# A float32 encoder trunk on one core: the first pair of feed-forward output tiles by eight plain block products instead of seven Winograd ones, with the input loaded in another order

## The chip, the cores and the metric

The kernel runs on 1 core of one Trainium2 chip, as one launch. The metric is device microseconds of that launch, the median of several runs. Engine names: PE is TensorE (its weight loads are PEld), DVE is VectorE, ACT is ScalarE, POOL is GpSimd, SP is SyncE, which here only issues transfers.

## What is computed

A two-layer encoder over 512 tokens of 1024 channels, all in float32. Only the first feed-forward block and the norm ahead of it are touched by the change:

```
for l in range(2):
    h = rmsnorm(x, ffn1_norm[l])
    x = x + 0.5 * (silu(h @ w_gate) * (h @ w_up)) @ w_down      # 1024 -> 2816 -> 1024
    ... mixer: windowed pooling, a 2-D Fourier transform, differential attention; x = x + concat @ w_out
    ... a second SwiGLU block of the same shape
out = rmsnorm(x, final_norm)
```

## The kernel before

The input lies transposed: eight tiles `X[k]` of 128 channels by 512 tokens. Every product is float32 made of three passes: an operand is split into a rounded part `hi` (ACT, line 103) and the remainder `lo` (DVE, line 104), and hi·hi, hi·lo and lo·hi are accumulated in PSUM. The norm's factor per token is not applied to the input of a product. Only the gain per channel is (`scaled`); the sums of squares run beside it (`squared`), and `end` makes the factor `r` by a reciprocal square root written out in DVE operations.

**Units.** A feed-forward block has 2816 / 128 = 22 hidden tiles, taken in pairs: a `Unit` computes the gate and up columns of one pair. It is a 2x2 block product. The blocks of the weights are a11, a12, a21, a22 (rows: the two tiles of the pair; columns: even and odd `X[k]`), each 128x1024 values or 512 KB, and those of the input are the halves `c0` (tokens 0 to 255) and `c1` (256 to 511) of even and odd `X[k]`. Seven Winograd products replace the eight plain ones. Each product is 24 matmuls of 128x256 (line 386 to 388: four pairs `p`, gate and up, three passes), so a unit is 168 matmuls. Its operands are sums of blocks. On the input's side `PairNorm.scaled` makes them on ACT and DVE once for all 11 units. On the weights' side transfers make them: a block is loaded by SP, and GpSimd issues a transfer that adds a second block onto it in SBUF (line 160 for a sum from the start, line 175 for the next sum once the tile has been split). So one tile `t` of a unit holds a21+a22, then that plus a11, then that plus a12.

**Order.** A list of raw tiles and a list of recipes are made ahead (which raw tile is split when, and what is added onto it then). `load` issues transfers up to five raw tiles ahead into 7 stage buffers; `produce` splits; `operand` keeps the splits three ahead of PE in 4 buffers. A unit is `head` (products 5 and 1), then the unit before it ends (`tail`), then `middle`; PSUM's 8 banks are given out in turn. Four units (chunk one of 4, 4 and 3) are followed by the down products `dn`. In the code all this stands in program order; a planner inside the framework then writes each engine's queue from that order and from its own estimate of when operands are ready, and each queue runs strictly in order.

**Start.** SP loads the small constants, then `X[0]`, `X[1]`, a11 of unit 0, `X[2]`, `X[3]`, the first tile `t`, and the rest. For the first unit products 1 and 5 are swapped, since product 1 needs the plain block a11 alone. After its `head` eight squares go to ACT and six of their seven additions to POOL.

Of the kernel before, what the change touches and what calls it, by code (L numbers as in the profile page):

```python
# [33 lines left out]
P = 128  # L34
D = 1024
S = 512
# [30 lines left out]
def build(tc, xt, gu, dn, qk, wv, wfa, wo, pw, fw, small, lamv, alibi, dft_c, dft_s, out):  # L67
# [3 lines left out]
    with (  # L71
# [50 lines left out]
        for l in range(L):  # L122
            for n in range(2):
                i = 2 * l + n
                if n:
                    src = {f"P{h}": qk[l, h] for h in range(NH)}
                    src |= {"V0": wv[l, 0], "V1": wv[l, 1], "A": wfa[l, 1], "F": wfa[l, 0]}
                    src |= {"W0a": wo[l, 0], "W1a": wo[l, 1], "W2": wo[l, 2], "W3": wo[l, 3]}
                    for x in ORDER:
                        if x in src:  # L130
                            for z in range(2):
                                operand_of(raw(src[x][:, z * 1024 : (z + 1) * 1024]), eng=V if x in ON_VECTOR else G)
                for c0, c1 in CHUNKS:
                    tail = []
                    for u in range(c0, c1):
                        a11, a21, a22, a12 = [gu[i, u][:, q * 1024 : (q + 1) * 1024] for q in range(4)]
                        if raws:
                            t, t11 = raw(a21, plus=a22), raw(a11)
                        else:
                            t11, t = raw(a11), raw(a21, plus=a22)  # L140
                        t12, t22 = raw(a12), raw(a22)
                        head = [(t, a11), (t11, a21)]
                        for x, then in (head if recipes else head[::-1]) + tail + [(t, a12), (t11, None), (t12, None)]:
# [114 lines left out]
        class Norm:  # L258
# [13 lines left out]
            def squared(self, k):  # L272
# [4 lines left out]
                else:  # L277
                    (V if k == KT - 1 else G).tensor_tensor(self.acc, self.acc, sq, ADD)
# [7 lines left out]
        class PairNorm(Norm):  # L286
# [6 lines left out]
            def scaled(self, k):  # L293
# [5 lines left out]
                b1, b2 = self.b.pop(k - 1), self.b.pop(k)  # L299
                c0, c1 = slice(0, TH), slice(TH, S)  # L300
# [13 lines left out]
                self.x[k // 2] = res  # L314
# [57 lines left out]
        class Unit:  # L372
# [5 lines left out]
            def product(self, q, j, start, stop):  # L378
                wh, wl = operand()
# [10 lines left out]
            def head(self, swapped=False):  # L390
                self.qe, self.qa = bank("qe"), bank("qa")
                for q, j in ((self.qa, 1), (self.qe, 5)) if swapped else ((self.qe, 5), (self.qa, 1)):
                    self.product(q, j, True, True)
# [36 lines left out]

        def ffn(nm, nxt, first=False):
            for c0, c1 in CHUNKS:
                act, last = [], None
                for u in range(c0, c1):
                    unit = Unit(nm)
                    unit.head(first and u == 0)
                    if first and u == 0:
                        for k in range(KT):
                            nm.squared(k)
# [315 lines left out]
        pos[2] = 1  # L755
        for k in range(KT):
            nm.scaled(k)
# [104 lines left out]
```

## Time and profile before

| | |
|---|---|
| median of 3 runs | 1875.59 us (1872.73 to 1879.64) |
| the profiled execution | 1877.81 us, of which span 1876.0 us |
| mean granted TensorE clock | 0.982 of full speed |
| PE busy | 1774.7 us of the span |
| DVE, ACT, POOL busy | 1360.3, 851.9, 320.6 us |
| moved by transfers | 265.01 MB, mean 141 GB/s |

The span runs from the first to the last instruction of the profiled execution; the 1.8 us beside it lie outside. A busy PE counts matmuls that overlap, so that the number of matmuls in a stretch and the distance between their starts say more than the busy share.

### The profile page before, as it was taken

To read this page: it belongs to the slowest core of one execution; us is meant where nothing else is said; L and a number is where in the kernel's file an instruction comes from. 1 tells how busy PE (TensorE), PEld (TensorE's weight loads), DVE (VectorE), ACT (ScalarE), POOL (GpSimd) and SP (SyncE) were. 2 spreads that over 40 slices of the span, in tenths; PEclk is the share of its full clock that TensorE was granted. 3 is DMA by queue.
4 is the path that set the end of the run, shared out by engine and by line. 5 is a ranking of instruction groups with operands and counts; after the bars stand their busy time and mean duration, and the time that the engine had idled before them with its cause. 6 is when DMAs were issued, how large, how long until landed. Compare 5 with 4: busy or idle time off the path is not lost.

```text
span 1876.0 us, 27955 instructions
## 1 busy us (share of the span) xinstructions
PE 1774.7 (95%) x11225; PEld 1603.5 (85%) x11225; DVE 1360.3 (73%) x1956; ACT 851.9 (45%) x1189; POOL 320.6 (17%) x282
## 2 busy tenths in 40 slices
PE   5899999999879999999999999999996989999997
PEld 4898989987668999989989899898775889899896
DVE  6675765789779874855798567478987897567474
ACT  6342533448545442534555234243773554244243
POOL 3101101032322101101031010113232220010101
PEclk9899999999989999999999999999998999999998
DMA  8666867532213866857678577573322267586561
GB/s 231 150 169 137 204 165 156 138 120 85 65 42 78 188 161 147 211 151 155 161 154 195 142 167 189 129 180 124 93 71 56 65 140 197 128 193 177 127 166 45
DMA packets 76738, 265.01 MB, mean 141 GB/s; under 512 B 8640, under 2 KB 10688, under 8 KB 76608
## 3 DMA queue, kind: packets, MB, share of 16 engines
q0 software_dynamic: 25344, 92.29, 29.1%
q1 hardware_dynamic: 48096, 167.25, 27.7%
q10 hardware_dynamic: 3168, 3.68, 0.7%
q8 instruction: 88, 1.44, 0.3%
q14 instruction: 42, 0.34, 0.1%
HBM read 261.09 MB, written 2.10 MB: 140 GB/s over the span
## 4 chain that ended last, share of the span: by engine, by line
PE 69%; DVE 12%; issue 7%; DMA 5%; ACT 5%; POOL 2%; SPq 0%; DVEq 0%; ACTq 0%; POOLq 0%
PE dn L107 7%; PE dn L108 7%; PE dn L109 7%; DMA st<-in_gu 5%; PE qg L386 4%; PE qg L387 4%; PE qg L388 4%; PE qe L386 3%; PE qe L387 3%; PE qe L388 3%; PE qa L388 3%; PE qa L386 3%; PE qa L387 3%; DVE lo L104 2%; ACT hi L103 2%
## 5 line engine op out<-in xcount | busy, mean ns | idle before, releaser
L103 ACT ACTIVATE hi<-st 128x1024 fp32r<-128x1024 f32 (+2 forms) x455 | 469.2, 1036 | 668.0 <-PE dn L108 214.8
L104 DVE TENSOR_TENSOR lo<-st,hi 128x1024 fp32r<-128x1024 f32 (+2 forms) x423 | 511.5, 1213 | 179.4 <-ACT hi L103 178.3
L108 PE MATMUL dn<-al,hi 128*128 128x512 f32 x704 | 274.6, 390 | 0.0
L109 PE MATMUL dn<-ah,lo 128*128 128x512 f32 x704 | 274.1, 389 | 0.0
L107 PE MATMUL dn<-ah,hi 128*128 128x512 f32 x704 | 272.1, 392 | 0.8
L175 POOL DMA_DIRECT2D st<-in_gu x132 | 120.7, 914 | 680.3 <-DVE lo L104 606.2
L386 PE MATMUL qe<-xh,hi 128*128 128x256 f32 x704 | 203.3, 289 | 20.0 <-ACT hi L103 10.3
L386 PE MATMUL qg<-xh,hi 128*128 128x256 f32 x704 | 201.3, 286 | 8.1 <-DVE w L404 7.7
L387 PE MATMUL qe<-xh,lo 128*128 128x256 f32 x704 | 202.6, 288 | 2.2 <-DVE lo L104 2.2
L388 PE MATMUL qe<-xl,hi 128*128 128x256 f32 x704 | 202.1, 287 | 1.8 <-DVE xl L104 1.8
L387 PE MATMUL qg<-xh,lo 128*128 128x256 f32 x704 | 200.8, 285 | 2.8 <-DVE lo L104 2.8
L388 PE MATMUL qg<-xl,hi 128*128 128x256 f32 x704 | 200.6, 285 | 0.0
L452 DVE SCALAR_TENSOR_TENSOR x<-dn,x 128x512 f32<-128x512 f32 x96 | 66.1, 689 | 163.2 <-PE dn L109 163.2
L107 PEld LDWEIGHTS dn<-ah,hi 128*128 128x128 f32 x704 | 131.3, 188 | 33.1 <-ACT ah L103 7.1
L386 PEld LDWEIGHTS qe<-xh,hi 128*128 128x128 f32 x704 | 137.9, 196 | 23.9 <-ACT hi L103 16.0
L108 PEld LDWEIGHTS dn<-al,hi 128*128 128x128 f32 x704 | 132.2, 188 | 29.0 <-DVE al L104 2.4
L109 PEld LDWEIGHTS dn<-ah,lo 128*128 128x128 f32 x704 | 132.2, 188 | 26.8
L386 PEld LDWEIGHTS qg<-xh,hi 128*128 128x128 f32 x704 | 136.4, 194 | 9.4 <-DVE w L404 7.6
L387 PEld LDWEIGHTS qe<-xh,lo 128*128 128x128 f32 x704 | 137.9, 196 | 4.0 <-DVE lo L104 3.1
L388 PEld LDWEIGHTS qe<-xl,hi 128*128 128x128 f32 x704 | 138.0, 196 | 2.4 <-DVE xl L104 2.0
L387 PEld LDWEIGHTS qg<-xh,lo 128*128 128x128 f32 x704 | 136.5, 194 | 3.0 <-DVE lo L104 3.0
L388 PEld LDWEIGHTS qg<-xl,hi 128*128 128x128 f32 x704 | 136.6, 194 | 0.0
(252 smaller groups left out, 3979.1 us busy)
## 6 DMA issues: line engine op xcount, KB each, us to landing
st<-in_gu SPq DMA_DIRECT2D x176, 512.0 KB, 4.5
st<-in_gu POOLq DMA_DIRECT2D x176, 512.0 KB, 5.6
st<-in_dn SPq DMA_DIRECT2D x64, 512.0 KB, 4.3
st<-in_dn SPq DMA_DIRECT2D x32, 384.0 KB, 3.3
st<-in_qk SPq DMA_DIRECT2D x16, 512.0 KB, 3.6
st<-in_wo SPq DMA_DIRECT2D x16, 512.0 KB, 3.7
st<-in_wv SPq DMA_DIRECT2D x8, 512.0 KB, 3.9
st<-in_wfa SPq DMA_DIRECT2D x8, 512.0 KB, 3.7
```

The costliest lines, as they stand in the source:

```text
L103: A.activation(hi, src, AF.Copy)
L104: (lo_eng or V).tensor_tensor(lo, src, f(hi), SUB)
L107: T.matmul(o, lh, rh, start=start, stop=False)
L108: T.matmul(o, lh, rl, start=False, stop=False)
L109: T.matmul(o, ll, rh, start=False, stop=stop)
L175: G.dma_start(t[:, 0:w], then, accum_op=ADD)
L386: T.matmul(o, wh[:, s], xh, start=start and p == 0 and z == 0, stop=False, **k)
L387: T.matmul(o, wl[:, s], xh, start=False, stop=False, **k)
L388: T.matmul(o, wh[:, s], xl, start=False, stop=stop and p == NK - 1 and z == 1, **k)
L452: V.scalar_tensor_tensor(X[m], b, 0.5, X[m], MUL, ADD)
```

## The change

The first unit becomes a `FirstUnit`. It multiplies the four plain weight blocks with plain halves of the input, eight products of 24 matmuls: a11 with even `X`, a12 with odd `X`, a21 with even, a22 with odd, each with `c0` and `c1`. Its weight blocks need no added transfers, and each is split once. The plain halves of the input are scaled and split directly from `X` (`plain`, 16 of them, each an ACT and a DVE operation of 128x256); twelve of them stay and serve the later units, four are used by the first unit alone. The operands that are sums (`sums`, by `joined`) are made in program order behind the first unit's first two products. The squares stand behind its last product, with all additions on DVE instead of six on POOL; `end` and the multiplication by `r` stand in its `tail`. SP's order is: constants, a11, the `c0` halves of the four even `X` (128 KB each), their `c1` halves, a12, the four odd `X` whole, a21, a22, and then the second unit's tiles. All other units are as before.

```diff
-                        if raws:
-                            t, t11 = raw(a21, plus=a22), raw(a11)
-                        else:
-                            t11, t = raw(a11), raw(a21, plus=a22)
+                        if not raws:
+                            for x in (a11, a12, a21, a22):
+                                operand_of(raw(x))
+                            continue
+                        t, t11 = raw(a21, plus=a22), raw(a11)
...
-        for k in range(KT):
+        load(1)
+        for c in range(2):
+            for k in range(0, KT, 2):
+                nc.sync.dma_start(X[k][:, c * TH : (c + 1) * TH], xt[k][:, c * TH : (c + 1) * TH])
+        load(2)
+        for k in range(1, KT, 2):
             nc.sync.dma_start(X[k], xt[k])
-            if k % 2:
-                load(min(k // 2 + 1, 2 + (k > 6)))
+        load(RAWS)
...
-            def squared(self, k):
+            def squared(self, k, eng=G):
...
-                    (V if k == KT - 1 else G).tensor_tensor(self.acc, self.acc, sq, ADD)
+                    (V if k == KT - 1 else eng).tensor_tensor(self.acc, self.acc, sq, ADD)
...
+                self.x[k // 2] = self.joined(b1, b2)
+
+            def joined(self, b1, b2, res=None):
                 c0, c1 = slice(0, TH), slice(TH, S)
                 ta, tb = g(name="ta"), g(name="tb")
                 V.tensor_tensor(ta[:, c0], b1[:, c0], b1[:, c1], SUB)
                 V.tensor_tensor(ta[:, c1], b1[:, c1], b2[:, c1], SUB)
                 V.tensor_tensor(tb[:, c0], ta[:, c1], b1[:, c0], SUB)
                 V.tensor_tensor(tb[:, c1], b2[:, c0], tb[:, c0], ADD)
-                one = g(F32R, name="xo")
-                split(b1[:, c0], one[:, c0], one[:, c1])
-                res = {1: (one[:, c0], one[:, c1])}
-                for src, js in ((ta, (5, 7)), (tb, (6, 4)), (b2, (2, 3))):
+                src = [(ta, (5, 7)), (tb, (6, 4))]
+                if res is None:
...
+                for src, js in src:
                     hi, lo = g(F32R, name="xh"), g(F32R, name="xl")
                     split(src, hi, lo)
                     for j, c in zip(js, (c0, c1)):
                         res[j] = hi[:, c], lo[:, c]
-                self.x[k // 2] = res
+                return res
+
+            def plain(self, k, c):
+                gain = sm[:, self.c + k : self.c + k + 1]
+                s, c0, c1 = slice(c * TH, (c + 1) * TH), slice(0, TH), slice(TH, S)
+                o = g(F32R, name="xo")
+                A.activation(o[:, c0], X[k][:, s], AF.Copy, scale=gain)
+                V.scalar_tensor_tensor(o[:, c1], X[k][:, s], gain, f(o[:, c0]), MUL, SUB)
+                j = (1, 0)[c] if k % 2 == 0 else (2, 3)[c]
+                self.x.setdefault(k // 2, {})[j] = o[:, c0], o[:, c1]
+
+            def sums(self, p):
+                b = [g(name="xg") for _ in range(2)]
+                for z in range(2):
+                    k = 2 * p + z
+                    A.activation(b[z], X[k], AF.Copy, scale=sm[:, self.c + k : self.c + k + 1])
+                self.joined(*b, self.x[p])
...
+        class FirstUnit(Unit):
+            def head(self):
+                self.c = [[bank("qc") for _ in range(2)] for _ in range(2)]
+                for js, n in (((1, 0), True), ((2, 3), False)):
+                    w = operand()
+                    for q, j in zip(self.c[0], js):
+                        self.product(q, j, n, not n, w)
+                    if n:
+                        for p in range(NK):
+                            self.nm.sums(p)
+            def middle(self):
+                for js, n in (((1, 0), True), ((2, 3), False)):
+                    w = operand()
+                    for q, j in zip(self.c[1], js):
+                        self.product(q, j, n, not n, w)
+                for x in self.nm.x.values():
+                    del x[0]
+                for k in range(KT):
+                    self.nm.squared(k, V)
+            def tail(self):
+                self.nm.end()
+                res = []
+                for q in self.c:
+                    t = halves(wide("t"))
+                    for i in range(2):
+                        s = slice(i * TH, (i + 1) * TH)
+                        r = self.nm.r[:, s].unsqueeze(1).to_broadcast([P, 2, TH])
+                        V.tensor_tensor(t[:, :, s], halves(q[i]), r, MUL)
+                    res.append(self.hidden(t))
+                return res
...
         nm = PairNorm(C_FFN1)
         produce(0, NK)
-        pos[2] = 1
-        for k in range(KT):
-            nm.scaled(k)
+        for c in range(2):
+            for k in range(0, KT, 2):
+                nm.plain(k, c)
+        produce(1)
+        for c in range(2):
+            for k in range(1, KT, 2):
+                nm.plain(k, c)
+        pos[2] = 2
```

## Rows read from the trace of the kernel before

**Rows 1.** The head of the profile's page.
```profile
span 1876.0 us, 27955 instructions
```

**Rows 2.** Busy time by hundreds of microseconds: stretch and its length, busy time (and instructions) of PE, PEld, DVE, ACT, POOL, then the granted clock, the share of the transfer engines and GB/s.
```profile
0.00:100.00 100.00, 71.41 (x471) 67.19 (x472) 67.68 (x99) 47.49 (x70) 23.01 (x29) 0.91 0.76 189
100.00:200.00 100.00, 99.85 (x656) 91.30 (x656) 60.74 (x73) 37.13 (x43) 8.97 (x11) 1.00 0.67 161
...
400.00:500.00 100.00, 90.70 (x415) 72.52 (x414) 86.69 (x187) 71.02 (x131) 31.47 (x17) 1.00 0.27 82
500.00:600.00 100.00, 86.10 (x404) 70.45 (x402) 81.63 (x157) 46.17 (x84) 24.06 (x17) 0.93 0.28 64
```

**Rows 3.** The same columns for the stretches of the start, and for the first 131.5 us in all; the last row is that of the tile `dn` alone (PE, PEld and DVE).
```profile
0.00:8.20 8.20, 2.50 (x5) 1.49 (x5) 4.09 (x12) 4.26 (x8) 0.99 (x8) 1.00 0.74 206
8.20:23.70 15.50, 3.91 (x12) 2.86 (x12) 8.09 (x18) 7.60 (x16) 1.93 (x2) 1.00 1.05 344
23.70:41.80 18.10, 16.06 (x108) 15.33 (x108) 13.94 (x21) 14.95 (x25) 6.94 (x7) 1.00 0.76 170
41.80:56.70 14.90, 9.97 (x43) 8.91 (x42) 10.28 (x10) 2.11 (x3) 7.07 (x6) 0.66 0.75 167
56.70:81.50 24.80, 24.80 (x207) 24.60 (x205) 19.94 (x25) 11.10 (x13) 4.35 (x5) 1.00 0.74 162
81.50:91.00 9.50, 5.16 (x27) 5.00 (x26) 2.52 (x3) 1.54 (x2) 0.00 (x0) 0.64 0.52 134
...
0.00:131.50 131.50, 102.83 (x705) 97.05 (x706) 91.21 (x129) 60.61 (x86) 24.74 (x31) 0.94 0.74 188
...
0.00:131.50 131.50, 6.38 (x26) 4.85 (x27) 0.00 (x0) 0.94 0.74 188
```

**Rows 4.** PE's timeline: start, duration, line, operation, out<-in, and in brackets the idle time before it and what ended it.
```profile
28.35 0.41 PE L386 MATMUL qe<-xh,hi 128*128 128x256 f32 x1
28.56 0.41 PE L387 MATMUL qe<-xh,lo 128*128 128x256 f32 x1
...
29.39 0.28 PE L386 MATMUL qa<-xo,hi 128*128 128x256 f32 x1
29.51 0.28 PE L387 MATMUL qa<-xo,lo 128*128 128x256 f32 x1
...
81.38 0.28 PE L388 MATMUL qe<-xl,hi 128*128 128x256 f32 x1
86.00 0.58 PE L386 MATMUL qg<-xh,hi 128*128 128x256 f32 x1 [4.34 <-DVE w L404]
...
90.44 0.32 PE L388 MATMUL qg<-xl,hi 128*128 128x256 f32 x1
```

**Rows 5.** Pieces of the chain that ended last, in the start: start, duration, what. A `DMA` piece runs from issue to landing.
```profile
2.13 5.65 DMA st<-in_gu
...
10.74 11.84 DMA st<-in_gu
...
25.22 5.61 DMA st<-in_gu
...
68.63 14.30 DMA st<-in_gu x2
```

**Rows 6.** The additions of squares in the start: count, shortest/median/longest in ns, first and last start in us.
```profile
L278 POOL TENSOR_TENSOR sq<-sq,sq x6: 1283/1551/2147, 37.4 to 47.7; 128x512 f32<-128x512 f32 x6
L278 DVE TENSOR_TENSOR sq<-sq,sq x1: 692/692/692, 49.0 to 49.0; 128x512 f32<-128x512 f32 x1
```

**Rows 7.** The first transfers: SP's issue of `X[0]` and `X[1]` and the ACT operation that waited for `X[0]`, from the timeline; then two stretches with the columns of rows 2 (the last numbers are the share of the transfer engines and GB/s).
```profile
1.19 0.90 SPq L194 DMA_DIRECT2D x<-in_xt  x2
...
3.98 0.72 ACT L296 ACTIVATE xg<-x,sm 128x512 f32<-128x512 f32 x1 [1.75 <-DMA x<-in_xt]
...
5.00:6.00 1.00, 0.00 (x0) 0.00 (x0) 0.44 (x2) 1.00 (x2) 0.00 (x0) 1.00 0.80 248
...
9.00:10.00 1.00, 1.00 (x5) 0.87 (x5) 0.99 (x4) 1.00 (x3) 0.00 (x0) 1.00 1.03 406
```

**Rows 8.** DVE's timeline where it ran without idle time.
```profile
23.70 1.23 DVE L104 TENSOR_TENSOR lo<-st,hi 128x1024 fp32r<-128x1024 f32 x1 [6.93 <-ACT hi L103]
24.84 0.42 DVE L104 TENSOR_TENSOR xo<-xg,xo 128x256 fp32r<-128x256 f32 x1
...
26.38 0.69 DVE L104 TENSOR_TENSOR xl<-xg,xh 128x512 fp32r<-128x512 f32 x1
26.98 0.42 DVE L302 TENSOR_TENSOR ta<-xg 128x256 f32<-128x256 f32 x1
27.32 0.42 DVE L303 TENSOR_TENSOR ta<-xg,xg 128x256 f32<-128x256 f32 x1
```

**Rows 9.** Timelines of DVE and ACT: the last addition of squares, the last operation of `r`, and the wait at 83 us.
```profile
48.98 0.69 DVE L278 TENSOR_TENSOR sq<-sq,sq 128x512 f32<-128x512 f32 x1 [2.53 <-POOL sq L278]
...
61.60 0.68 DVE L249 SCALAR_TENSOR_TENSOR y<-t,y 128x512 f32<-128x512 f32 x1
...
83.03 1.06 ACT L103 ACTIVATE hi<-st 128x1024 fp32r<-128x1024 f32 x1 [6.14 <-DMA st<-in_gu]
...
84.12 1.23 DVE L104 TENSOR_TENSOR lo<-st,hi 128x1024 fp32r<-128x1024 f32 x1 [4.57 <-ACT hi L103]
85.26 0.68 DVE L404 TENSOR_TENSOR w<-qg,v 128x512 f32<-128x512 f32 x1
```

More of the change, by code (lines that the diff above doesn't have):

```diff
@@ L136, in build @@
                         a11, a21, a22, a12 = [gu[i, u][:, q * 1024 : (q + 1) * 1024] for q in range(4)]
-                        if raws:
-                            t, t11 = raw(a21, plus=a22), raw(a11)
-                        else:
-                            t11, t = raw(a11), raw(a21, plus=a22)
+                        if not raws:
[3 more added lines that the diff above has]
+                        t, t11 = raw(a21, plus=a22), raw(a11)
                         t12, t22 = raw(a12), raw(a22)
-                        head = [(t, a11), (t11, a21)]
-                        for x, then in (head if recipes else head[::-1]) + tail + [(t, a12), (t11, None), (t12, None)]:
+                        for x, then in [(t, a11), (t11, a21)] + tail + [(t, a12), (t11, None), (t12, None)]:
                             operand_of(x, then=then)
@@ L305, in scaled @@
                 V.tensor_tensor(tb[:, c1], b2[:, c0], tb[:, c0], ADD)
-                one = g(F32R, name="xo")
-                split(b1[:, c0], one[:, c0], one[:, c1])
-                res = {1: (one[:, c0], one[:, c1])}
-                for src, js in ((ta, (5, 7)), (tb, (6, 4)), (b2, (2, 3))):
+                src = [(ta, (5, 7)), (tb, (6, 4))]
+                if res is None:
+                    one = g(F32R, name="xo")
+                    split(b1[:, c0], one[:, c0], one[:, c1])
+                    res = {1: (one[:, c0], one[:, c1])}
+                    src.append((b2, (2, 3)))
+                for src, js in src:
                     hi, lo = g(F32R, name="xh"), g(F32R, name="xl")
@@ L376, in __init__, with product @@
                 self.nm = nm
-            def product(self, q, j, start, stop):
-                wh, wl = operand()
+            def product(self, q, j, start, stop, w=None):
+                wh, wl = w or operand()
                 k = {"skip_group_check": True}
@@ L388, in product @@
                         T.matmul(o, wh[:, s], xl, start=False, stop=stop and p == NK - 1 and z == 1, **k)
-            def head(self, swapped=False):
+            def head(self):
                 self.qe, self.qa = bank("qe"), bank("qa")
-                for q, j in ((self.qa, 1), (self.qe, 5)) if swapped else ((self.qe, 5), (self.qa, 1)):
-                    self.product(q, j, True, True)
+                self.product(self.qe, 5, True, True)
+                self.product(self.qa, 1, True, True)
                 self.q1 = g(name="q1")
@@ L434, in ffn @@
                 for u in range(c0, c1):
-                    unit = Unit(nm)
-                    unit.head(first and u == 0)
-                    if first and u == 0:
-                        for k in range(KT):
-                            nm.squared(k)
+                    unit = FirstUnit(nm) if first and u == 0 else Unit(nm)
+                    unit.head()
                     if last:
```

2 lines of the change are left out of this document (1 added, 1 removed).

## The prediction, made before the changed kernel was run

> **What bounds the kernel now.** The profiled execution's span is 1876.0 us [rows 1]. I read the busy time by hundreds of microseconds first [rows 2]. From 100 us on PE is nearly always busy in the feed-forward stages (99.85 of 100 us). The first 100 us have only 71.41. The change edits this start alone, so I made a ledger of it. Up to 131.5 us PE loaded weights 706 times [rows 3]: 5 for warming up, 2 for the sum of squares, 27 for `dn`, and so 672, which is four units of 168. At its quick pace a 128x256 matmul starts every 0.12 us (29.39 to 29.51 [rows 4]). Then the four units are worth 672 x 0.12 = 80.6 us, `dn` 6.4 [rows 3], the sum of squares about 0.5: 87.5 of 131.5 us. So 44.0 us are lost at the start, and this is all that the change can touch.
>
> The stretches [rows 3] say where, each as its length less 0.12 us per matmul: 8.2 us before the first product; 14.1 up to 23.7, in which only 12 products ran; 5.1 up to 41.8; 9.5 up to 56.7; nothing up to 81.5; 6.3 up to 91. The sum, 43.2, is within a microsecond of the ledger.
>
> The chain of waits names the causes [rows 5]. The first a11 took 5.65 us to land. The added transfer that makes the first `t` took 11.84, the next one alone 5.61. Two added transfers for a later unit took 14.30. At 83 us [rows 9] ACT waited 6.14 us for such a tile, DVE's split stood behind ACT, and `w`, which had its inputs, stood behind that split in DVE's queue; PE's next product waited 4.34 us for `w` [rows 4]. One late tile stops three queues.
>
> A gap also costs what follows it. After the gap that ended at 86.00, matmuls started about 0.21 us apart until 90.44 (4.44 / 0.21 = 21 of them), 0.09 us more each than at the quick pace: 1.9 us. The granted clock of 81.5 to 91 is 0.64 [rows 3], a mixture of full and half speed, 2.4 and 1.2 GHz. The same slow pace stands at 28.35 to 28.56 [rows 4], and the quick one 0.83 us later, 5.7 us after work was taken up again at 23.7 [rows 3].
>
> **The change part by part.** *Matmuls.* Eight products for seven: 24 x 0.12 = +2.9 us.
>
> *Input and first blocks.* No row shows a transfer of 128 KB with rows of 1 KB. While `X` came in pieces of 256 KB the engines moved 248 GB/s, while weight blocks of 512 KB came 406 [rows 7]: 1.05 us for the one, 1.29 for the other, so 256 KB more cost 0.24, and a half piece by the same line takes 1.05 - 0.12 = 0.93. Bounds: 0.52 (the rate of the whole ones) and 1.05 (no gain from halving). I take 0.93, since the two sizes measured differ so little in time. `X[0]`, issued at 1.19, was used at 3.98: 2.8 us. With a11 in its place and 0.24 more, a11 lands near 4.3. SP issues every 0.45 us (two in 0.90), so it keeps ahead. Estimated landings: `c0` halves at 5.2, 6.1, 7.1, 8.0; `c1` halves by 11.7; a12 at 13.0; odd `X` at 14.1, 15.1, 16.2, 17.2; a21 at 18.5; a22 at 19.8; the second unit's `t` at 21.
>
> The Trainium skill, page "DMA: Bandwidth & Descriptors", section "Measured (HBM→SBUF, 128 partitions, SWDGE, issued from GpSimd)", advises against this edit: it wants 1 MiB or more per transfer. The page's fit for one transfer issued by GpSimd, 2.0 us plus bytes over 436 GB/s, gives an estimate of 2.3 us for a half piece that nothing overlaps; eight would take 18.4 us, and the sum would be some 11 us worse. The trace shows no transfer of this size alone, only several in flight together.
>
> *First unit on PE.* A plain half needs one ACT and one DVE operation, 0.42 us each by the nearest row [rows 8], so the first product starts near 5.7. Its 24 matmuls at the slow pace, 0.21 us, last to 10.8; the quick pace comes, as it did after 23.7, within 5.7 us of the start, so by 11.4. The second product ends at 14.0. a12's products follow the odd `X`: with 0.8 us for the plain operations and 0.72 for the last six matmuls of a half, 17.2 + 1.5 = 18.7, then 2.9 more: 21.6. a21 and a22 are split by then (19.8 + 1.23 + 1.06 = 22.1 for a22, wanted at 27.4). The unit ends at 33.1. It is worth 192 x 0.12 = 23.0, so 10.1 us are lost here.
>
> *Second unit's head.* Its `t` is whole when an added transfer has landed on it: 21 + 5.6 to 11.8 [rows 5] = 26.6 to 32.8, then ACT and DVE. I take 30 to 32, and a wait of 1 us: head from 34.1 to 39.9, product 6 to 42.8. The four added transfers that the first unit had (one for its sum, three later ones) are gone, which keeps GpSimd's queue clear.
>
> *DVE.* Here the rest of the old wait goes. PE's fifth product needs `qg`, whose bank is one of the first unit's four (one for the warm-up, four, two for the head, one for the sum of squares, and the ring of 8 is through with product 6). It is free when DVE has multiplied it by `r`. At back-to-back spacings of 0.34, 0.60 and 1.14 us for 256, 512 and 1024 columns [rows 8], DVE's work from the first odd `X` at 14.1: eight plain halves 2.7; splits of a21 and a22 2.3; sums, 4 x (4 x 0.34 + 2 x 0.60) = 10.2; splits of three tiles of the next unit 3.4; seven additions of squares 4.2; two more splits 2.3; the split of the sum and the wait for its matmuls 1.8; nine operations of `r` 5.4; the multiplication 0.6. Sum 32.9, so 47.0. Before, `r` came at 61.60 + 0.68, 12.6 us behind the last addition's end [rows 9]. PE waits 47.0 - 42.8 = 4.2 us, and like the gap at 86.00 this costs 1.9 more at the slow pace. Six of the additions took 1.55 us each on POOL [rows 6]; the move costs DVE 6 x 0.60 = 3.6 us of the 4.2 and takes them out of the queue that issues the added transfers.
>
> *Sum.* Lost after: 10.1 + 1 + 4.2 + 1.9 = 17.2. Gain: 44.0 - 17.2 - 2.9 = 23.9 us, and the profiled execution would go from 1877.81 to 1853.9. That execution lies 2.2 above the median, which gives 1851.7 beside the median. I leave about 3 us for small waits in units two and three that the sum does not list and say 1855. After 131 us nothing is taken to change: PE is busy, and a gain at the start passes through.
>
> **The rivals.** *Nothing waits after the start.* DVE's additions fit into its pauses and product 2, which needs no new bank, is put ahead of `qg`. With `X` at 248 GB/s only 8.3 us are lost: gain 44.0 - 8.3 - 2.9 = 32.8, about 1843 beside the median. For it: DVE has pauses while the odd `X` land. Against: 32.9 us of DVE work in 33. Chance 0.13.
>
> *The second unit's sum holds ACT.* The planner puts its split ahead of the `sums`, as the first `t`'s split stood for 7 us at the head of ACT's queue before 22.6 (its DVE part waited 6.93 us [rows 8]). The sum lands at 32.8; DVE then still has three of four sums (7.7) and the later terms (20.0): 32.8 + 27.7 = 60.5. PE: head until 43, product 6 to 46, then a gap of 14 and some 4 us of slow pace. Lost 10 + 4 + 14 + 4 = 32: gain 9, 1867. Chance 0.17.
>
> *Small pieces do not overlap.* Each half takes 2.8 us from issue to landing [rows 7] one after the other, 8 x 2.8 = 22.4 for 7.4: gain 23.9 - 15.0 = 8.9, 1867. This is how the page's advice would show here. Against it: SP issues every 0.45 us while 248 GB/s already come in. Chance 0.05.
>
> *Slower.* The planner writes every queue anew, and the mixers, where all engines depend on one another, lose 9.3 and 13.9 us in 400 to 600 [rows 2]. A worse order in one of them would have to lose 33 us more to be 0.5% slower, that is to more than double its wait; below 24 us the kernel stays faster. For it: queues are not in program order. Against: the mixer's order is written out, and a shift by a constant changes few of the planner's comparisons. Chance 0.05.
>
> **How the numbers follow.** The forecast has 0.60. 0.5% (9.4 us) is about what a measurement of this kernel can tell from no change. The forecast, the first rival and half of the second (0.09), with 0.02 of the third, are faster by more: 0.84. The rest of the second and third, 0.11, lie within; 0.05 slower. The range goes from the first rival's 1843 to the second's 1867, which leaves out the slower case and the ends beyond, under 2 in 10.
>
> **What would show it right or wrong.** In the changed profile: the first product before 6 us; the quick pace by 12; 192 matmuls without a gap over 2 us, ended by 34; transfers of `X` of 128 KB near 0.9 us apart; the first multiplication by `r` near 47 and a gap of some 4 us just before the second unit's `qg`; no stretch like 81.5 to 91. `dn` would begin about 24 us earlier than before. The prediction is wrong if ACT stands for several microseconds before the second unit's first split with `sums` behind it, or if the start gains and a mixer gives it back.

## The result, and the profile after

The changed kernel takes 1865.03 us (median of 5 runs, 1862.69 to 1868.55), the kernel before 1877.48 beside it (1872.73 to 1879.64): a ratio of 0.9939, 95% interval 0.9917 to 0.9960. That is 12.45 us faster, inside the forecast's range and on its side, but 8 us short of the 20.6 that 1855 meant. The profiled execution took 1862.69 us, its span 1860.9.

Busy time in the hundreds and stretches of the kernel after, with the columns of [rows 2, 3]:

```profile
0.00:100.00 100.00, 83.81 (x604) 81.11 (x605) 76.97 (x120) 55.06 (x83) 11.51 (x20) 0.93 0.74 198
...
400.00:500.00 100.00, 92.69 (x420) 73.64 (x418) 84.88 (x197) 71.28 (x136) 30.99 (x19) 0.98 0.28 80
500.00:600.00 100.00, 83.84 (x441) 70.89 (x442) 86.48 (x150) 52.18 (x90) 24.50 (x17) 0.95 0.31 69
...
0.00:7.30 7.30, 2.50 (x5) 1.49 (x5) 2.83 (x10) 3.22 (x8) 0.99 (x8) 1.00 0.71 214
7.30:33.10 25.80, 25.75 (x193) 25.71 (x194) 19.06 (x37) 17.39 (x31) 3.61 (x4) 1.00 0.98 313
33.10:40.00 6.90, 3.80 (x32) 3.60 (x30) 4.74 (x9) 4.89 (x7) 0.86 (x1) 1.00 0.69 129
40.00:44.00 4.00, 3.78 (x17) 3.48 (x17) 2.35 (x4) 1.58 (x2) 0.00 (x0) 0.57 1.01 218
44.00:48.70 4.70, 0.00 (x0) 0.00 (x0) 4.15 (x6) 4.70 (x11) 0.00 (x0) 0.84 0.47 149
48.70:57.60 8.90, 8.22 (x35) 7.74 (x36) 7.46 (x11) 1.62 (x3) 1.73 (x2) 0.51 0.69 118
57.60:106.10 48.50, 45.86 (x377) 45.19 (x376) 41.57 (x53) 24.93 (x30) 4.31 (x5) 1.00 0.64 163
```

PE's first hundred rose from 71.41 to 83.81 us. The start now has three parts: 25.8 us in which unit one runs without a gap, 24.5 us (33.1 to 57.6) with two gaps and two stretches at about half clock, and a clean rest. The two hundreds of the mixer together hold 176.5 us of PE, 176.8 before: nothing was given back there. The first `dn` matmul moved from 119.5 to 106.1 us, 13.4 earlier, and the last one of the program from 1859.8 to 1844.9, 14.9 earlier.

PE's timeline, each start that had waited over half a microsecond after unit one (columns as in [rows 4]):

```profile
40.04 0.39 PE L414 MATMUL qe<-xh,hi 128*128 128x256 f32 x1 [3.14 <-ACT xh L103]
48.80 0.58 PE L414 MATMUL qa<-xo,hi 128*128 128x256 f32 x1 [4.98 <-ACT q L423]
51.46 0.80 PE L258 MATMUL ss<-g,ones 128*128 128x512 f32 x1 [0.58 <-ACT g L103]
64.02 0.36 PE L414 MATMUL qe<-xh,hi 128*128 128x256 f32 x1 [1.55 <-DVE t L490]
71.19 0.39 PE L414 MATMUL qg<-xh,hi 128*128 128x256 f32 x1 [1.08 <-ACT hi L103]
```

Both large gaps end with ACT: the split of a sum of x (`xh`), and `q1`, a copy out of PSUM that takes 0.57 us. ACT's timeline says why such small things were late:

```profile
27.51 1.06 ACT L103 ACTIVATE hi<-st 128x1024 fp32r<-128x1024 f32 x1 [4.57 <-PE qc L416]
28.48 0.62 ACT L103 ACTIVATE xh<-ta 128x512 fp32r<-128x512 f32 x1
...
35.78 1.06 ACT L103 ACTIVATE hi<-st 128x1024 fp32r<-128x1024 f32 x1 [1.35 <-DMA st<-in_gu]
36.74 1.32 ACT L341 ACTIVATE xg<-x,sm 128x512 f32<-128x512 f32 x2
38.41 1.06 ACT L103 ACTIVATE hi<-st 128x1024 fp32r<-128x1024 f32 x1 [0.35 <-DMA st<-in_gu]
39.37 0.61 ACT L103 ACTIVATE xh<-ta 128x512 fp32r<-128x512 f32 x1
...
43.05 1.06 ACT L103 ACTIVATE hi<-st 128x1024 fp32r<-128x1024 f32 x1 [1.32 <-PE qa L416]
44.01 4.25 ACT L278 ACTIVATE sq<-x 128x512 f32<-128x512 f32 x8
48.17 0.57 ACT L423 ACTIVATE q<-qa 128x512 f32<-128x512 f32 x1
```

The `hi` operations are splits of the second unit's blocks. The one at 27.51 had to have the added transfer of its sum, which POOL issued at 18.11 and which took 9.3 us. (Its row names PE, whose sixth product ended within 0.1 us of that landing. PE is not what it needs: in e8 below the same split ran at 26.39, right behind an earlier landing and ahead of that product's end.) The splits at 35.78 and 38.41 wait for the next added transfers, which POOL can issue only when the low parts of the first two splits are done. The splits of the sums of x stand behind them, the squares behind those, and `q1` behind the squares. DVE, fed by ACT, went the same way:

```profile
45.28 5.46 DVE L282 TENSOR_TENSOR sq<-sq,sq 128x512 f32<-128x512 f32 x7
...
53.37 0.69 DVE L233 TENSOR_SCALAR v<-ss 128x512 f32<-128x512 f32 x1 [0.89 <-PE ss L259]
...
63.19 2.48 DVE L490 TENSOR_TENSOR t<-qc,y 128x512 f32<-128x512 f32 x4
```

The additions of squares begin at 45.28, the first multiplication by `r` at 63.19 (forecast: 47.0), and a bank that it frees is what the third unit's head gets at 64.02.

### The profile page after: what moved, and what is told of

It is laid out like the page before. It is cut to its first block, busy times and chain, and to the rows that moved or that the text cites. A ratio compares the mean times of both kernels' runs of the same rounds, so it can differ in the third digit from the quotient of the medians.

```text
span 1860.9 us, 28011 instructions
## 1 busy us (share of the span) xinstructions
PE 1773.0 (95%) x11249; PEld 1604.4 (86%) x11249; DVE 1355.0 (73%) x1962; ACT 853.6 (46%) x1193; POOL 307.2 (17%) x272
## 4 chain that ended last, share of the span: by engine, by line
PE 78%; DVE 11%; ACT 4%; DMA 3%; issue 3%; POOL 0%; DVEq 0%; ACTq 0%; SPq 0%; POOLq 0%
PE dn L107 8%; PE dn L108 7%; PE dn L109 7%; PE qg L414 4%; PE qg L415 4%; PE qg L416 4%; PE qe L414 4%; PE qe L415 4%; PE qe L416 4%; PE qa L416 4%; PE qa L415 4%; PE qa L414 4%; DMA st<-in_gu 3%; DVE lo L104 2%; PE qb L415 2%
## 5 line engine op out<-in xcount | busy, mean ns | idle before, releaser
L104 DVE TENSOR_TENSOR lo<-st,hi 128x1024 fp32r<-128x1024 f32 (+2 forms) x420 | 505.4, 1206 | 179.2 <-ACT hi L103 178.2
L175 POOL DMA_DIRECT2D st<-in_gu x129 | 116.0, 903 | 656.7 <-DVE lo L104 546.7
L414 PE MATMUL qg<-xh,hi 128*128 128x256 f32 x688 | 197.4, 287 | 9.0 <-DVE w L432 7.9
L415 PE MATMUL qg<-xh,lo 128*128 128x256 f32 x688 | 196.7, 286 | 0.0
L416 PE MATMUL qg<-xl,hi 128*128 128x256 f32 x688 | 196.7, 286 | 0.0
L414 PE MATMUL qe<-xh,hi 128*128 128x256 f32 x608 | 173.3, 285 | 14.6 <-ACT xh L103 8.4
L415 PE MATMUL qe<-xh,lo 128*128 128x256 f32 x608 | 172.5, 284 | 2.1 <-DVE lo L104 2.1
L416 PE MATMUL qe<-xl,hi 128*128 128x256 f32 x608 | 172.4, 283 | 1.8 <-DVE xl L104 1.8
L414 PEld LDWEIGHTS qe<-xh,hi 128*128 128x128 f32 x608 | 116.7, 192 | 17.9 <-ACT xh L103 9.2
L414 PE MATMUL qa<-xo,hi 128*128 128x256 f32 x424 | 120.9, 285 | 5.0 <-ACT q L423 5.0
L416 PE MATMUL qa<-xo,hi 128*128 128x256 f32 x424 | 121.3, 286 | 2.8 <-DVE xo L104 2.8
```

The lines of the kernel that those rows point to most:

```text
L104: (lo_eng or V).tensor_tensor(lo, src, f(hi), SUB)
L175: G.dma_start(t[:, 0:w], then, accum_op=ADD)
L414: T.matmul(o, wh[:, s], xh, start=start and p == 0 and z == 0, stop=False, **k)
L415: T.matmul(o, wl[:, s], xh, start=False, stop=False, **k)
L416: T.matmul(o, wh[:, s], xl, start=False, stop=stop and p == NK - 1 and z == 1, **k)
```

## The experiments

Every kernel below is the kernel after with an edit, timed beside runs of the kernel before. This table is worked out from their traces and times; the third unit's head is PE's start of its `qe`.

| kernel | first multiplication by `r` | third unit's head | first `dn` | last `dn` | median, us | ratio to before (95%) |
|---|---|---|---|---|---|---|
| after | 63.2 | 64.0 | 106.1 | 1844.9 | 1865.0 | 0.9939 (0.9917 to 0.9960) |
| e1_sums_first | 62.3 | 63.1 | 104.9 | 1846.6 | 1862.3 | 0.9925 (0.9904 to 0.9945) |
| e2_copy_first | 62.0 | 62.9 | 105.0 | 1848.3 | 1866.3 | 0.9951 (0.9933 to 0.9968) |
| e3_both | 63.6 | 64.4 | 106.5 | 1847.4 | 1866.7 | 0.9951 (0.9934 to 0.9969) |
| e4_sq_pool | 65.7 | 66.6 | 108.7 | 1847.0 | 1865.7 | 0.9955 (0.9936 to 0.9974) |
| e5c_r_ahead | 57.1 | 57.9 | 99.6 | 1841.2 | 1859.6 | 0.9917 (0.9903 to 0.9931) |
| e7c_all | 55.9 | 56.8 | 98.7 | 1837.3 | 1856.5 | 0.9904 (0.9889 to 0.9920) |
| e8_x_whole | 59.1 | 59.9 | 102.0 | 1841.5 | 1861.1 | 0.9926 (0.9912 to 0.9940) |
| e9_order | 62.6 | 63.4 | 106.2 | 1842.8 | 1861.4 | 0.9930 (0.9917 to 0.9943) |
| e10_best | 59.4 | 60.3 | 104.6 | 1840.7 | 1860.7 | 0.9909 (0.9886 to 0.9931) |
| e11_nopool | 55.2 | 56.1 | 98.2 | 1835.2 | 1857.4 | 0.9887 (0.9863 to 0.9911) |
| e12_old_loads | 62.5 | 63.3 | 106.3 | 1847.7 | 1862.9 | 0.9913 (0.9888 to 0.9938) |
| e13_r_first | 51.0 | 51.8 | 103.2 | 1844.6 | 1861.7 | 0.9921 (0.9903 to 0.9939) |

Two regularities run through it. In eleven of the thirteen kernels the first `dn` comes 41.7 to 43.0 us behind the third unit's head (44.3 in e10, 51.4 in e13; the reason for the latter is below). And from the first to the last `dn` it takes 1736.1 to 1743.3 us (before: 1740.3): what the start gains arrives at the end, with some 3.6 us either way. Each trace is one execution, and the five runs of the kernel after alone lie 5.9 us apart. So a median that differs by 4 us says little by itself; the start is read from the trace. A trace has its own spread: in the seven kernels with unchanged loads (after, e1 to e4, e5c, e9) the first product starts at 7.35 to 7.99, so half a microsecond between two traces says nothing.

**e1, e2, e3: one wait taken away, then the other.** My first theory was that ACT's order alone costs the two gaps. e1 queues the second unit's splits behind the last split of a sum of x; e2 queues the squares behind `q1`; e3 does both.

```diff
--- e1
...
-            A.activation(hi, src, AF.Copy)
+            if behind:
+                with tc.issue_after(behind[0]):
+                    i = A.activation(hi, src, AF.Copy)
...
-                split(t[:, s], hi[:, s], lo[:, s], eng)
+                split(t[:, s], hi[:, s], lo[:, s], eng, last_sum if 4 <= i <= 7 else None)
--- e2
-                for k in range(KT):
-                    self.nm.squared(k, V)
 
             def tail(self):
+                with tc.issue_after(getattr(self.copy, "ins", self.copy)):
+                    for k in range(KT):
+                        self.nm.squared(k, V)
                 self.nm.end()
```

> Edit: ACT's splits of recipes 4 to 7 (the second unit's first tiles) are queued behind the last split of the input sums; nothing else. Anchor in the changed kernel: the first dn product at 106.1 us, second unit's head 33.1 to 43.8 with a gap of 3.1. Theory A (ACT's queue order costs the missing gain): the sums are done near 31, the head runs 33.1 to 38.9 without a gap and without slow matmuls, 4.9 us gained, part of the gap before product 2 too since the squares move ahead of a waiting split; first dn at 98 to 101, 1857 to 1860. Theory B (DVE's work up to r is the bound, as forecast): the head gains but the wait moves to the multiplication by r near 63; first dn stays at 105 to 106, 1863 to 1866. Theory C (the missing gain lies in later stages): first dn may move, the time does not follow.

> Edit: the eight squares on ACT are queued behind the second unit's copy q1; nothing else. Theory A: the gap of 5.0 us that ended at 48.8 goes, and the slow matmuls after it are fewer; r comes no more than 1 us later; first dn at 98 to 101, 1857 to 1860. Theory B: r sets the pace, so the wait moves to the third unit's head: first dn at 105 to 107, 1863 to 1866. Theory C: as for the kernel before this one.

> Edit: both orders together (splits of the second unit behind the sums, squares behind q1). Theory A: both gains add: about 9 to 12 us of the start, first dn at 94 to 98, 1852 to 1857. Theory B: r is now made from 39 on and cannot come before 50 to 53; the third unit's head waits for it, first dn at 99 to 104, 1858 to 1863.

PE's waits in e1 up to 110 us (for what, on whom, us, times, longest):

```profile
PE qa L422 <- ACT q L431: 7.4, 1, 7.4
PE qe L422 <- DVE t L499: 3.9, 1, 3.9
```

In e1 the head's wait is gone, and `q1` is late by 7.4 us: it stands behind a split at 42.48 that waits for an added transfer. In e2 the wait before `qa` fell to 0.8, and the matmuls that add up the squares wait 4.4 us for the split of their sum. In e3 `q1` (5.4) and that split (2.8) are late together. `r` came at 62.0 to 63.6 in all three, and the first `dn` at 104.9 to 106.5. The theory of the two waits falls: taking either away only shows the next, as long as `r` stays where it is. For e3 theory B missed as well: it had `r` early once both waits were gone (first `dn` at 99 to 104), and `r` did not move.

**e4: the squares' additions back on POOL**, all else as in the kernel after.

```diff
-                    self.nm.squared(k, V)
+                    self.nm.squared(k)
```

> Edit: six of the seven additions of squares back on POOL, as in the kernel before; all else as in the changed kernel. Nine microseconds on POOL for four on DVE put r some 5 us later. Theory B: the start ends 3 to 6 us later, first dn at 109 to 112, 1868 to 1871. Theory A: the gap before product 2 stays as it is (the squares stand on ACT as before) and r was waited for by 1.6 us only, so 2 to 5 us later by that wait alone, first dn at 108 to 111. If r does not matter at all: 106, 1865.

Six additions took 8.00 us on POOL, 44.46 to 52.46, and the seventh on DVE waited for them; `r` came 2.5 us later and the first `dn` 2.6. The move to DVE is worth that at the start, less than the spread of the runs, and the median doesn't show it.

**e5c and e9: `r` out of the chained splits' queue.** The theory now: `r` is late because `q1`, the last square and its split stand behind the splits of the chained sums, that is of the tiles onto which a further block was added. In e5c the second unit takes its plain a12 product third, the chained splits go behind `q1` and the split of the sum of squares on ACT, and behind the first of the nine operations of `r` (the Newton steps) on DVE. e9 has the new order of products without these two queue edits. Both keep e1's edit, here for the second unit's first five splits, and so do e7c, e10, e11 and e13.

```diff
--- e5c and e9
+                        if i == 0 and u == 1:
+                            rest = rest[2:] + rest[:2]
...
+                if self.early:
+                    self.product(self.qa, 2, False, True)
                 self.product(self.qb, 6, True, True)
--- e5c
+                for n in (7, 8):
+                    for j in (self.nm.g[0], inst(self.copy)):
+                        queue_behind(his[n][0], j)
+                    queue_behind(his[n][1], newton[0])
```

> Edit: in the second unit the product from a12 and its plain split are ordered third, ahead of the two products that use the chained sums; on ACT the splits of those chained sums are queued behind the copy q1 and the split of the sum of squares, and on DVE their low parts behind the first Newton operation of r; the splits of the sums of x go first. Theory (r is late because q1, the last square and its split stand in ACT's and DVE's queues behind splits that wait for the chained added transfers): no wait over 1.5 us before the second product into qa (7.4 in the run with the sums first), q1 at about 41, r's last operation done by 54 (62.3 there), third unit's head at 55 (63.1 there), first down product at about 98 (104.9 there; 106.1 in the kernel after), time 1857, 1853 to 1861. Rival (the chained transfers themselves bind): the product into qb can't start before its low part, TensorE waits 3 to 6 us there instead, third unit's head at 60 or later, first down product 103 to 106, time 1862 to 1867.

> Edit: the sums of x first and the second unit's a12 product third, but one split of a chained sum still stands ahead of q1 on ACT and the next ahead of the split of the sum of squares, as the planner puts them. Theory of the queues: q1 stays behind that split, at 42 to 45, a wait of 3 to 5 us before the second product into qa remains, r's first use at 58 to 62, first down product at 102 to 105, time 1861 to 1865; only the queue edit of its sister run brings the rest. Rival (the order of the products alone matters): as good as the sister run within 2 us at the first down product.

e5c, PE's waits:

```profile
PE qe L430 <- DVE t L514: 6.0, 1, 6.0
...
PE qg L430 <- ACT hi L108: 1.2, 1, 1.2
PE qa L430 <- ACT q L439: 0.7, 1, 0.7
```

`q1` ran at 40.13, `v` at 43.84, `r` was used at 57.1, six microseconds earlier than in the kernel after; first `dn` 99.6, time 1859.6 (expected 98 and 1857). In e9 ACT has both chained splits still ahead of `q1`:

```profile
42.39 1.06 ACT L108 ACTIVATE hi<-st 128x1024 fp32r<-128x1024 f32 x1 [3.10 <-DMA st<-in_gu]
46.38 1.06 ACT L108 ACTIVATE hi<-st 128x1024 fp32r<-128x1024 f32 x1 [2.93 <-DMA st<-in_gu]
47.34 0.58 ACT L434 ACTIVATE q<-qa 128x512 f32<-128x512 f32 x1
```

PE waits 6.2 us for it, and the first `dn` comes at 106.2, as in the kernel after. So the place in the queue is the cause, and not the order of the products. The wait at the third unit's head remains, and it names DVE: six low parts of 1.22 us, the two chained ones and four more, stand between the nine operations of `r`.

**e7c, e8, e11, e12: the loads.** e7c adds to e5c that the second unit's a21 is loaded ahead of the first unit's a21 and a22; e8 is the kernel after with even `X` whole; e11 has all of this; e12 is the kernel after with the old order of loads.

```diff
--- e8, e11
-        for c in range(2):
-            for k in range(0, KT, 2):
-                nc.sync.dma_start(X[k][:, c * TH : (c + 1) * TH], xt[k][:, c * TH : (c + 1) * TH])
+        for k in range(0, KT, 2):
+            nc.sync.dma_start(X[k], xt[k])
--- e7c, e11
-                            for x in (a11, a12, a21, a22):
-                                operand_of(raw(x))
+                            first = [raw(a11), raw(a12)]
...
+                            early = raw(n21, plus=n22)
+                            for x in first + [raw(a21), raw(a22)]:
+                                operand_of(x)
--- e12
-        load(1)
...
+        for k in range(KT):
+            nc.sync.dma_start(X[k], xt[k])
+            if k % 2:
+                load(min(k // 2 + 1, 2 + (k > 6)))
```

> Edit: the same order, and SP loads the second unit's a21 ahead of the first unit's a21 and a22, so that the added transfer that makes its sum starts about 3 us earlier. Theory of the queues alone: the same as without the earlier load within 3 us, 1857, since r comes from squares that need no sum. Rival (the added transfers bind): whatever waits for a sum goes 3 us earlier, third unit's head 3 us or more ahead of the run without the earlier load, first down product at 95 or earlier, time 1853. Against both: the first unit's a21 comes one block (1.3 us at the rate of whole blocks) later, at about 20, and the first unit's third pair of products starts there; if it stops, unit one ends later than 33.1 by that much.

> Edit: the even tiles of X are loaded whole (four transfers of 256 KB) in place of eight halves of 128 KB. By the prediction's price per piece (0.93 us a half, 1.05 a whole tile) the even tiles are all there 8 x 0.93 - 4 x 1.05 = 3.2 us earlier, a12 and the odd tiles too, and the first column halves 0.1 to 0.5 us later. If a half costs in truth about half a whole tile, the odd tiles land at the same time as in the kernel after (13.9), and the fourth first-column half 1 to 2 us later. By either, TensorE is paced by its own slow clock until 13, so unit one ends within 0.5 us of 33.1 and the time is the kernel after's, 1860 to 1868.

> Edit: the same without POOL: a12 product third, chained splits behind r, a21 early, X whole. By the loads alone everything behind them comes 1.1 us earlier than in the run with the first three edits (the added transfer's issue moves by that when X is whole): r's first multiplication at 54.8, third unit's head at 55.7, first down product at 97.6, time 1855. Rival: r hangs on the squares, which hang on ACT's queue and not on the loads, and nothing moves: 56.8, 98.7, 1856.5.

> Edit: the kernel after, with x loaded as in the kernel before (eight whole tiles in order, weight blocks between them); the eight plain products and all else stay. If the order of need is what lets the first unit start, as the prediction has it, the first product waits for the fourth even tile, behind 2.75 MB at 250 to 400 GB/s and the first 2 us: 9 to 13; the first product stops there for up to 3 us, unit one ends at 34 to 36, first down product at 107 to 109, time 1866 to 1869. If the plain products alone do it (the slow pace of TensorE, 1.28 us for each tile's six, hides the later tiles), unit one ends within 1 us of 33.1 and, with whole pieces, the time is that of the run with whole tiles, 1859 to 1863.

SP's issue of the even tiles and the rate of all transfers at 9 us in the kernel after, halves:

```profile
1.65 4.23 SPq L196 DMA_DIRECT2D x<-in_xt  x8
...
9.00:10.00 1.00, 1.00 (x7) 1.00 (x7) 1.00 (x4) 1.00 (x3) 0.00 (x0) 1.00 0.89 287
```

and in e8, whole tiles:

```profile
1.66 1.85 SPq L195 DMA_DIRECT2D x<-in_xt  x4
...
9.00:10.00 1.00, 1.00 (x7) 1.00 (x6) 0.83 (x3) 1.00 (x3) 0.00 (x0) 1.00 1.04 404
```

Eight halves take SP 4.23 us to issue, four whole tiles 1.85, so that a12 behind them is issued at 5.93 in place of 3.55. The even tiles themselves do not come later for it: the halves landed 0.35 to 0.43 us apart, the last at 8.55, the last whole tile at 8.82. What is slower comes behind them. At 9 us a12 and the odd tiles move in both kernels, at 287 GB/s in the kernel after and 404 in e8; a12 landed at 11.2 for 10.1, the last odd tile at 13.9 for 12.8. Why these same blocks move more slowly behind halves is not shown. With whole tiles POOL issues the first added transfer 1.15 us earlier (16.96 for 18.11); unit one ends later by 0.4 us, and `r` and the first `dn` come 4.1 earlier. I expected nothing of this edit. The second unit's splits, which wait for the transfers, run 1.1 us earlier (26.39 for 27.51). The rest of the 4.1 comes with another order of ACT's queue, which the planner wrote too:

```profile
26.39 1.06 ACT L103 ACTIVATE hi<-st 128x1024 fp32r<-128x1024 f32 x1 [4.32 <-DMA st<-in_gu]
...
40.56 4.25 ACT L277 ACTIVATE sq<-x 128x512 f32<-128x512 f32 x8
44.72 1.04 ACT L103 ACTIVATE hi<-st 128x1024 fp32r<-128x1024 f32 x1
```

The squares stand ahead of the split at 44.72, of a12, which ran ahead of them at 43.05 in the kernel after.

Whole tiles bring e11 0.5 us at the first `dn` against e7c, between its two expectations and within the spread of traces, and the early a21 brings e7c 0.9 against e5c: once `r` is ahead of the chained splits, the loads weigh little.

e12 has its first product at 8.80 and unit one's last matmul at 36.9, 4 us later than the kernel after. The order of need does what the forecast wanted of it in unit one: in e8, with whole tiles in that order, the last matmul comes at 33.3. And yet e12 has the same first `dn` (106.3) and no worse time. Its waits for the split of a sum of x and for `q1` are shorter, 1.8 and 1.1 us for 3.1 and 5.0, and `r` came at 62.5, for 63.2 in the kernel after. But e12 undoes two things at once, the order and the halves, and its squares stand ahead of the split of a12 as in e8. Beside e8, from which it differs in the order alone, its first `dn` is 4.3 us later, while the intervals of the two ratios overlap. So what the order won at the start, the halves and the queue that came with them lost: the load edit as a whole is worth nothing here.

**e10 and e13: the low parts off `r`'s way.** e10 is e11 with the next three blocks' low parts on POOL; e13 is e11 with them behind the multiplications by `r` on DVE.

```diff
--- e10
-            recipes.append((t, w, eng, then))
+            recipes.append((t, w, G if len(recipes) in (9, 10, 11) else eng, then))
--- e13
+                if 9 <= i <= 11:
+                    queue_behind(his[i][1], mults[{9: 0, 10: 1, 11: 3}[i]])
+                    if i < 11:
+                        queue_behind(mults[i - 8], his[i][1])
```

> Edit: the second unit's a12 product third, both chained splits queued behind r, its a21 loaded early, X whole, and besides the low parts of the next three weight blocks on POOL in place of DVE. Theory (r's last operations are now held up on DVE by those three low parts of 1.22 us each, 47 to 55 us): r's first multiplication moves from 55.9 (run with all three edits) to 51 to 52.5, third unit's head from 56.8 to 52 to 54.5, first down product from 98.7 to 94 to 96, time 1850 to 1854. Rival: POOL's low part (two of the 1551 ns additions for twice the columns, 3.1 us as an estimate) is later than DVE's was, and the third unit's second product waits for it; the gain is below 1 us and the time that of the run without POOL.

> Edit: as the run without POOL (a12 product third, chained splits behind r, a21 early, X whole), and on DVE the low parts of the next three weight blocks are queued behind r: the first behind the first multiplication with r, the second behind the one after, the third behind the last. Theory (four low parts between r's operations, 46.2 to 53.1, are all that keeps r late): r's seven remaining operations follow the two chained low parts without a gap, 45.6 + 7 x 0.70 = 50.5, the first multiplication at 50.5 in place of 55.2, third unit's head at 51.3 to 52.5 in place of 56, first down product at 94 to 95 in place of 98.2, time 1853, 1849 to 1857. Rival: the third unit's head then waits for its own low part (1.22 us after the multiplications, 53 to 54) and its next one; the first down product moves by less than 2 us and the time stays 1856 to 1859.

Timelines of e10, DVE and then POOL:

```profile
45.35 2.89 DVE L264 TENSOR_TENSOR t<-y 128x512 f32<-128x512 f32 x1
48.28 4.08 DVE L268 TENSOR_TENSOR t<-t,v 128x512 f32<-128x512 f32 x1
52.40 4.08 DVE L269 SCALAR_TENSOR_TENSOR y<-t,y 128x512 f32<-128x512 f32 x1
56.51 0.69 DVE L264 TENSOR_TENSOR t<-y 128x512 f32<-128x512 f32 x1
...
44.49 3.21 POOL L111 TENSOR_TENSOR lo<-st,hi 128x1024 fp32r<-128x1024 f32 x1 [9.87 <-ACT hi L110]
...
48.80 3.01 POOL L111 TENSOR_TENSOR lo<-st,hi 128x1024 fp32r<-128x1024 f32 x1
...
52.67 3.25 POOL L111 TENSOR_TENSOR lo<-st,hi 128x1024 fp32r<-128x1024 f32 x1
```

Three operations of `r` took 2.89, 4.08 and 4.08 us in place of 0.69, each while a subtraction ran on POOL, and ended about 0.5 us behind it; `r` came 4.2 us later than in e11. Neither expectation had this. In e13 `r` came at 51.0 and the third unit's head at 51.8, as expected, but the first `dn` at 103.2, 5 us later than in e11. PE waits, e13:

```profile
PE qg L438 <- ACT hi L110: 3.5, 1, 3.5
...
PE qb L438 <- ACT hi L110: 2.0, 1, 2.0
PE qe L438 <- DVE t L522: 1.1, 1, 1.1
```

and its POOL and ACT timelines:

```profile
53.70 0.86 POOL L200 DMA_DIRECT2D st<-in_gu  x1 [0.43 <-DVE lo L111]
...
61.65 1.06 ACT L110 ACTIVATE hi<-st 128x1024 fp32r<-128x1024 f32 x1 [4.65 <-DMA st<-in_gu]
```

A low part is not only an operand: the next added transfer writes over the block that it reads, so it can be issued only behind it. In e11 POOL issued that transfer at 47.73, in e13 at 53.70; it landed 8 us later, ACT's split waited for it, and PE stood before the third unit's `qb` and `qg`. Moved behind `r`, the low part made the chain of added transfers late. Neither expectation had this: the rival looked for the wait at the third unit's head and for an unchanged first `dn`. Two chains, `r` and the added transfers, both need DVE here; of the orders tried e11 and e7c have the earliest first `dn`, 98.2 and 98.7, and the lowest ratios, 0.9887 and 0.9904, though their intervals overlap those of several others.

## Why the prediction was right, and where it was not

*Right:* that all of the gain comes from the first 131 us, and that it passes through: 13.4 us at the first `dn`, 14.9 at the last, 12.45 in the medians. The 24 added matmuls are there. Unit one ran without a gap and ended at 33.2 (forecast 33.1), so 10.1 us are lost there, as forecast. The stall of 81.5 to 91 [rows 3, 9] is gone: the largest wait between 64.1 and 110 us is 1.08.

*Unit one, right by two errors that cancel.* a11 landed at 5.5, not 4.3, the first product started at 7.35, not 5.7, and the slow pace lasted to about 13, not 11.4; against that ACT used the last odd tile's first half at 13.9, where I had it land at 17.2. The price of 0.93 us for a half was too high, since the halves landed some 0.4 us apart, under its lower bound of 0.52; and a11 took 4.36 us from its issue, where I had put little more than the 2.8 of `X[0]`. From 7.35 on PE waited for nothing, so neither mattered.

*The term that failed: waits and slow pace behind unit one.* I had 1 for the head, 4.2 before `qg` and 1.9 of slow pace, 7.1 in all. The trace has idle 3.14 + 4.98 + 0.58 + 1.55 + 1.08 = 11.3. At the pitch of 0.21 us, 0.09 more than at the quick pace, 40.04 to 43.8 holds 17 matmuls of products (1.5 us) and 48.80 to 57.4 another 32 (2.9): 4.4. Together 15.7, so 8.6 of the 10.5 us by which 13.4 fell short of 23.9. Each gap of over 3 us was paid again by the clock, as the prediction said of the one at 86.00, but for two gaps in place of one.

*The step in it: "DVE's work from the first odd `X` at 14.1", without a pause, to `r` at 47.0.* `r` was used at 63.19, 16.2 later. DVE was busy 36.96 of the 49.10 us between, so my 32.9 of work was 4 short, and 12.1 were pauses, most of them in 22 to 44 us, when ACT's queue stood at the second unit's splits. The longest, 4.28 us before the low part at 28.60, is that of the first split. I had taken one wait of 1 us for the second unit's `t`, for PE alone, and none for the sums chained on it. The added transfer itself came inside its bounds: landed at 27.4, bounds 26.6 to 32.8. What sat behind it in ACT's queue was not counted, for it nor for the two that followed.

*That is the second rival's mechanism in good part*, and the sign that the prediction named for being wrong: the planner put the split ahead of the sums, and ACT stood 4.57 us before the second unit's first split at 27.51, with six of the eight splits of sums behind it. It then stood again before the next two, at 35.78 and 38.41. The rival's price, a gap of 14 us at one place, came as 3.1 and 5.0 at two. The time, 1865, lies near its 1867. So the range held because this rival set its upper end: the forecast's own path to `r`, without pauses, did not come about.

*The wait before `qg` was the wrong place.* I counted the banks as a ring, so that the second unit's `qg` would need a bank that `r` frees. It ran without a wait from 57.5 to 60.3, before the first multiplication by `r` at 63.19, so its bank did not hang on `r`. `r` binds at the third unit's head, where the trace shows `qe <-DVE t`. e5c, e7c, e8 and e11 show that this is what counts: their first `dn` follows it by 42 us. And a third of product 2, 8 of its 24 matmuls, did go ahead of the other two products, as the first rival supposed of all of it, only to wait for `q1`.

*The edits that I costed.* The squares on DVE: a gain of 2.6 us at the start (e4), where I had charged DVE 3.6: on POOL the additions end later still. The loads: halves and order together gave nothing at the first `dn` (e12); against whole tiles in the same order the kernel after is 4.1 us late there, 1.1 of it by the transfers (e8). What is left for the plain products themselves, with no added transfer ahead of unit one, is some 11 of the 13.4 us. That is an elimination; no run takes them back alone. The page "DMA: Bandwidth & Descriptors" of the Trainium skill (section "Measured (HBM→SBUF, 128 partitions, SWDGE, issued from GpSimd)") advises larger transfers, and its direction holds here for what is loaded behind the halves: the last odd tile landed 1.1 us later than in e8. The 11 us of the estimate from the page's fit are not in the trace, and the halves themselves were not late.

*Open:* the 1736 to 1743 us from the first to the last `dn`. Runs of one kernel differ by nearly as much (5.9 us in the kernel after, 6.4 in e7c), so one trace of each does not tell whether one set of queues is better than another there.

## What to carry to other kernels

When a gap ends with a small operation, read its engine's queue upwards to the operation that waits for memory, and then everything else that stands behind that one: here the reciprocal root of a norm, which needs no weight at all, came 16 us later than forecast behind splits of weights. Taking one wait away is a test only if the chain that sets the end moves with it; find the point behind which the rest is of constant length (here the third unit's head, 42 us ahead of the first `dn`) and judge each edit by that point. An operation that also releases a buffer for a transfer has two deadlines, and the transfer's can be the earlier one.

## What the runs showed of the hardware

The first added transfer of the kernel after got nothing at first, while SP's queue had the engines. The transfers of 18 to 22 us in the kernel after, queue by queue (packets, MB, share of 16 engines), and the issue in it (KB, us from issue to landing):

```profile
q1 hardware_dynamic: 446, 1.62, 101.0%
...
st<-in_gu POOLq DMA_DIRECT2D x1, 512.0 KB, 9.3
```

and those of 22 to 28 us:

```profile
q1 hardware_dynamic: 392, 1.37, 58.2%
q0 software_dynamic: 150, 0.55, 46.5%
```

The transfer issued at 18.11 moved nothing of its 512 KB in the first 4 us, while SP's queue moved 410 GB/s, and landed 9.3 us after its issue. With nothing in SP's queue one took 5.61 [rows 5].

A subtraction of 128x1024 on POOL stretched DVE's two-input operations of 128x512 from 0.69 to 2.89 and 4.08 us (e10). The Trainium skill, page "GPSIMD Engine Reference", section "Key points", says that POOL and VectorE share their SBUF interfaces and contend when a DVE instruction has two SBUF inputs; the trace agrees, and gives the size: 4.08 is 0.69 and 3.4 more, about the 3.0 to 3.25 us that the subtraction took.
